# A tile of ones multiplied 32 times into an unread bank at the head of a single-core DiT block

## The chip, the cores and the metric

The kernel is one program on one core of a Trainium2 chip. The metric is the device time of one execution in microseconds (us); a kernel's number is the median over its runs. In a profile, PE is TensorE's matmul side and PEld its weight load, DVE is VectorE, ACT is ScalarE, POOL is GpSimd, and SP is the engine whose queue issues nearly all the loads.

## The reference

One layer of a diffusion block over 1024 latent tokens of width 1024, with 256 context tokens, all in float32:

```
sh1, sc1, g1, sh2, sc2, g2 = split(silu(c) @ w_mod + b_mod, 6)      # the same with c_ctx for the context
h  = rmsnorm(x, norm1_w) * (1 + sc1) + sh1                          # hc from ctx likewise
k, v, ig, fg, q, o, xin, gate_c, gate_b, merge = split(h @ w_in + b_in)
y_a = (gate_b * conv3(gate_c * xin)) @ w_conv_out
y_b = (norm(mlstm(q, k, v, ig, fg, state of hc)) * sigmoid(o)) @ w_mlstm_out
x  = x + g1 * ((sigmoid(merge_a) * y_a + sigmoid(merge_b) * y_b) @ w_out)
x  = x + g2 * (relu(modulate(x, norm2_w, sh2, sc2) @ w_ff1) ** 2 @ w_ff2)
out = rmsnorm(x, final_norm_w)
```

## The kernel before

Features lie on the 128 partitions and tokens along the free axis. Every large product is made of three products of halves (`PASS`): each operand is split into a high part and the rest (`whi`/`wlo`, `hh`/`hl`), and hi*hi, hi*lo and lo*hi are added in one bank. The conv, mLSTM-output, output and MLP products are cut into blocks with fewer multiplications (the `Pairs` class and its `m1` to `m7`).

This case is about the head of the program, some 47 us. It does, all at once:

- loads. `m` in the list `ORDER` loads one of 16 tiles `wmod` (512 KB each, half of the adaLN weights for one block of features), `x` one of the token tiles, `w` the first projection weights `wst`, `v` the weights `v0s`, `k` and `l` the constants and rows (`cst`, `comb`, `gb`, `vb`). All are issued by SP through the helper `dma` (line 92), in the written order.
- adaLN. `mod_rows(k)` (`r` in `ORDER`) multiplies two `wmod` tiles with `sil32`, the silu of both conditioning vectors padded to 32 columns: four column groups of 32, each 256 wide, into a bank `pso`. `y` copies the result to `mrow` on DVE; `mod_cols` (`c`) turns it into per-feature columns with eight very small products against `comb` into the one bank `psu` (`mcol`), and DVE makes `mod1` of them.
- the norm. `square` and `hat` (`h`, `n`) make the normalised tokens `xh` on ACT and DVE; `transposed` (`f`) transposes them on PE against `cst`; `modulate` (`u`) and `j` make `hh` and `hl`.
- the first projection. `gemm_k` (`g`) adds feature block after feature block into two banks `psg` with the weights of `w`.

`ORDER` fixes the order on every engine and queue: with `pinned[0]` true, each instruction is kept in program order (`tc.keep_in_program_order`); outside it the scheduler may place it. From some 47 us on the program is a long stream of products.

`bank()` gives a PSUM bank of 512 columns from a rotating pool of three (`psg`) in this part; `page()` gives a slot of SBUF from a pool of 37.

The program's first instructions, ahead of the change:

Of the kernel before, what the change touches and what calls it, by code (L numbers as in the profile page):

```python
# [13 lines left out]
P = 128  # L14
# [19 lines left out]
)  # L34
MOD_RATE = 0.16
YC = 448

U_K, U_Q, U_O, U_X, U_GC, U_GB, U_MA, U_MB = 0, 4, 8, 16, 24, 32, 40, 48
NUNIT = 56
# [19 lines left out]
def tile_block(ctx: ExitStack, tc: tile.TileContext, x, cx, w_mod1, w_mod, w_v0, w_v, w_unit, w_conv, w_mls, w_o, w_f1, w_f2, cols_d, rows_d, cst_d, out):  # L59
    nc = tc.nc  # L60
    pinned = [False]
# [18 lines left out]
    V, A, G, PE, SY = Engine(nc.vector), Engine(nc.scalar), Engine(nc.gpsimd), Engine(nc.tensor), nc.sync  # L80
# [17 lines left out]
    def nm(s):  # L98
        uid[0] += 1
        return f"{s}_{uid[0]}"  # L100

    def page(shape, dt=F32, name="pg"):
        return pg.tile(shape, dt, tag="pg", name=nm(name))
# [90 lines left out]
    def bank(tag="g"):  # L194
        if tag == "g":
            pool = psg
            if psg2:
                pool = (psg, psg2[0])[turn[0] % 8 > 2]
                turn[0] += 1
            return pool.tile([P, 512], F32, tag="g", name=nm("psg"))  # L200
        return psm.tile([P, 512], F32, tag=tag, name=nm("ps" + tag), bufs=2 if tag == "o" else 1)
# [6 lines left out]
    sil32 = page([P, 8, 32], name="sil32")  # L208
    G.memset(sil32, 0.0)
    V.tensor_copy(sil32[:, :, 0:2], sil)  # L210

    eps_c = cpool.tile([P, 1], F32, name="eps_c")
    V.memset(eps_c, EPS)
# [1519 lines left out]
    for j in range(4):  # L1733
# [27 lines left out]
        V.reciprocal(rs[:, 1:2], rs[:, 0:1])  # L1761
        yc = YC if t == TT - 1 else D
        A.activation(y[:, :yc], xf[:, :yc], AF.Copy, scale=rs[:, 1:2])
# [91 lines left out]
```

## Time and profile before

| what | value |
|---|---|
| median of 3 runs | 1772.45 us (1772.2 to 1773.82) |
| the profiled execution | 1773.45 us, of which the span is 1771.7 us |
| PE busy | 1724.8 us, 97% of the span |
| DVE, ACT, POOL busy | 71%, 42%, 10% |
| DMA | 261.10 MB, mean 147 GB/s; in the first of 40 slices 358 GB/s |

The span runs from the first to the last instruction; the execution's own time is 1.75 us longer. A slice of the page is 44 us, so the whole head is its first slice. In tables of stretches, `PEclk` is the clock that TensorE was granted, as a share of full speed, and the DMA share is the mean busy share of the 16 DMA engines.

### The profile page before, as it was taken

To read this page: it belongs to the slowest core of one execution; us is meant where nothing else is said; L and a number is where in the kernel's file an instruction comes from. 1 tells how busy PE (TensorE), PEld (TensorE's weight loads), DVE (VectorE), ACT (ScalarE), POOL (GpSimd) and SP (SyncE) were. 2 spreads that over 40 slices of the span, in tenths; PEclk is the share of its full clock that TensorE was granted. 3 is DMA by queue.
4 is the path that set the end of the run, shared out by engine and by line. 5 is a ranking of instruction groups with operands and counts; after the bars stand their busy time and mean duration, and the time that the engine had idled before them with its cause. 6 is when DMAs were issued, how large, how long until landed. Compare 5 with 4: busy or idle time off the path is not lost.

```text
span 1771.7 us, 23486 instructions
## 1 busy us (share of the span) xinstructions
PE 1724.8 (97%) x8633; PEld 1427.8 (81%) x8633; DVE 1252.1 (71%) x2216; ACT 745.5 (42%) x1229; POOL 177.6 (10%) x265
## 2 busy tenths in 40 slices
PE   6999999999999999999999999999999999999994
PEld 4998989877878888888888878877888888888884
DVE  4367556474966679878889988876666656577785
ACT  4534453565333322222344435554443454343434
POOL 1102221312200000000000001110111000000001
PEclk9999999999999999999999999999999999999997
DMA  9124131332525454343747255144344285675352
GB/s 358 47 61 105 34 90 44 89 81 63 201 96 172 161 166 137 102 162 110 262 157 258 71 215 175 64 166 161 133 164 161 107 287 193 233 240 189 106 179 95
DMA packets 102243, 261.10 MB, mean 147 GB/s; under 512 B 11760, under 2 KB 24944, under 8 KB 102128
## 3 DMA queue, kind: packets, MB, share of 16 engines
q1 hardware_dynamic: 85808, 200.88, 35.1%
q0 software_dynamic: 16320, 58.73, 8.4%
q8 instruction: 67, 1.10, 0.3%
q14 instruction: 48, 0.39, 0.1%
HBM read 198.62 MB, written 60.95 MB: 147 GB/s over the span
## 4 chain that ended last, share of the span: by engine, by line
PE 67%; DVE 3%; ACT 2%; issue 1%; ACTq 0%; DVEq 0%
PE psg L73 67%; ACT y L73 1%; DVE wst L73 0%; ACT Fsh L73 0%; DVE y L73 0%; ACT fc L73 0%; DVE fc L73 0%; DVE wlo L73 0%; DVE x L73 0%; DVE ftmp L73 0%; DVE Ff L73 0%; DVE Fsl L73 0%; DVE ol L73 0%; DVE f L73 0%; ACT fd L73 0%
## 5 line engine op out<-in xcount | busy, mean ns | idle before, releaser
L73 DVE TENSOR_TENSOR wlo<-wst,whi 128x512 fp32r<-128x512 f32 (+1 forms) x236 | 221.3, 941 | 143.4 <-ACT whi L73 141.3
L73 ACT ACTIVATE whi<-wst 128x512 fp32r<-128x512 f32 (+1 forms) x238 | 196.0, 827 | 259.8 <-PE psg L73 166.0
L73 PE MATMUL psg<-wlo,whi 128*128 128x512 f32 (+2 forms) x688 | 266.6, 387 | 0.2 <-DVE wlo L73 0.2
L73 PE MATMUL psg<-whi 128*128 128x512 f32 (+2 forms) x688 | 265.9, 387 | 0.0
L73 PE MATMUL psg<-whi,wlo 128*128 128x512 f32 (+2 forms) x688 | 265.4, 386 | 0.0
L73 PE MATMUL psg<-hh,whi 128*128 128x512 f32 x440 | 175.8, 406 | 0.0
L73 PE MATMUL psg<-hl,whi 128*128 128x512 f32 x440 | 172.4, 398 | 0.0
L73 PE MATMUL psg<-hh,wlo 128*128 128x512 f32 x440 | 172.0, 397 | 0.0
L73 PEld LDWEIGHTS psg<-whi 128*128 128x128 f32 x688 | 129.3, 188 | 27.8
L73 PEld LDWEIGHTS psg<-wlo,whi 128*128 128x128 f32 x688 | 129.2, 188 | 27.4 <-DVE wlo L73 0.6
L73 PEld LDWEIGHTS psg<-whi,wlo 128*128 128x128 f32 x688 | 129.2, 188 | 27.1
L73 PEld LDWEIGHTS psg<-hh,wlo 128*128 128x128 f32 x440 | 83.0, 189 | 18.9 <-DVE wlo L73 0.2
L73 PEld LDWEIGHTS psg<-hh,whi 128*128 128x128 f32 x440 | 82.1, 188 | 19.1 <-issue 0.8
L73 PEld LDWEIGHTS psg<-hl,whi 128*128 128x128 f32 x440 | 83.1, 189 | 16.9
L73 PE MATMUL psg<-oh,Fsl 128*128 128x512 f32 x240 | 94.7, 394 | 0.1
L73 PE MATMUL psg<-oh,Fsh 128*128 128x512 f32 x240 | 94.6, 394 | 0.0
L73 PE MATMUL psg<-ol,Fsh 128*128 128x512 f32 x240 | 94.6, 394 | 0.0
L73 DVE TENSOR_TENSOR u<-psg,u 128x512 f32<-128x512 f32 x67 | 45.8, 687 | 51.4 <-PE psg L73 51.4
L73 PE MATMUL psg<-whi,hh 128*128 128x256 f32 (+1 forms) x256 | 76.1, 297 | 0.0
L73 PE MATMUL psg<-whi,hl 128*128 128x256 f32 (+1 forms) x256 | 73.1, 286 | 0.0
L73 PE MATMUL psg<-wlo,hh 128*128 128x256 f32 (+1 forms) x256 | 73.1, 286 | 0.0
L73 POOL TENSOR_TENSOR wqz<-w,q 64x256 f32<-64x256 f32 x64 | 49.1, 771 | 158.6 <-PE pso L73 137.0
(338 smaller groups left out, 3797.5 us busy)
## 6 DMA issues: line engine op xcount, KB each, us to landing
wst<-fq SPq DMA_DIRECT2D x112, 256.0 KB, 2.7
wst<-in_w_unit_dram SPq DMA_DIRECT2D x38, 512.0 KB, 5.1
mst<-in_w_mod_dram SPq DMA_DIRECT2D x32, 512.0 KB, 4.4
fq<-Ff POOLq DMA_DIRECT2D x32, 512.0 KB, 3.7
wst<-in_w_f_dram SPq DMA_DIRECT2D x64, 256.0 KB, 3.0
wst<-in_w_f_dram SPq DMA_DIRECT2D x21, 512.0 KB, 4.4
Hwst<-in_w_unit_dram SPq DMA_DIRECT2D x18, 512.0 KB, 5.5
wmod<-in_w_mod_dram SPq DMA_DIRECT2D x16, 512.0 KB, 8.5
```

What stands on the lines that cost most here:

```text
L73: i = f(*a, **kw)
```

## The change

After `sil32` is made, a page of 128 by 128 ones is filled on DVE, and PE multiplies it with itself 32 times into 128 columns of a bank that nobody reads. The 32 products are pinned in program order, so they are the first work on PE.

```
+HUM = 32
...
     G.memset(sil32, 0.0)
     V.tensor_copy(sil32[:, :, 0:2], sil)
+
+
+    busy = page([P, P], name="busy")
+    V.memset(busy, 1.0)
+    hum = bank()
+    pinned[0] = True
+    for _ in range(HUM):
+        PE.matmul(hum[:, 0:P], busy, busy, start=True, stop=True)
+    pinned[0] = False
```

TensorE at the start of the program, before (`pso` from `wmod` and `sil` is `mod_rows`, `psm` and `pso` from `cst` and `xh` are transposes, `psu` is `mod_cols`):

```order
L73 MATMUL pso_169<-wmod_165,sil_2_83 32x256 x4
L73 MATMUL pso_169<-wmod_132,sil_2_83 32x256 x4
L73 MATMUL pso_186<-wmod_167,sil_2_83 32x256 x4
L73 MATMUL pso_186<-wmod_181,sil_2_83 32x256 x4
L73 MATMUL psm_55_204<-cst_67,xh_152 128x128
```

and now:

```order
L74 MATMUL psg_88<-busy_86 128x128 x32
L74 MATMUL pso_204<-wmod_200,sil_2_83 32x256 x4
L74 MATMUL pso_204<-wmod_167,sil_2_83 32x256 x4
L74 MATMUL pso_221<-wmod_202,sil_2_83 32x256 x4
L74 MATMUL pso_221<-wmod_216,sil_2_83 32x256 x4
L74 MATMUL psm_57_239<-cst_67,xh_187 128x128
```

The 32 products stand ahead of the first `mod_rows`; what follows is the same work in the same order, with other buffer numbers.

VectorE at the start of the program, before:

```order
L73 MEMSET eps_c 128x1
L73 MEMSET ones_c 128x2
L73 TENSOR_SCALAR kb_108<-cols 128x4
L73 TENSOR_TENSOR sil<-cols,sig 128x16
L73 COPY sil_2_83<-sil 128x8x2
```

and now:

```order
L74 MEMSET eps_c 128x1
L74 MEMSET busy_86 128x128
L74 MEMSET ones_c 128x2
L74 TENSOR_SCALAR kb_143<-cols 128x4
L74 TENSOR_TENSOR sil<-cols,sig 128x16
L74 COPY sil_2_83<-sil 128x8x2
```

One fill more, second on the engine; all other rows of DVE, and all rows of ACT, POOL and SP, follow each other as before.

## The prediction, made before the changed kernel had run

> **What bounds the kernel now.** I read the page's heading and engine shares first, then the list of what PE waited for, then a table of stretches of the head, then the rows of PE, DVE and SP there in order of time.
>
> ```profile
> span 1771.7 us, 23486 instructions
> PE 1724.8 (97%) x8633; PEld 1427.8 (81%) x8633; DVE 1252.1 (71%) x2216; ACT 745.5 (42%) x1229; POOL 177.6 (10%) x265
> PE pso L73 <- DMA wmod<-in_w_mod_dram: 13.6, 2, 11.6
> PE psg L73 <- ACT u L73: 1.5, 2, 1.2
> ```
>
> PE is busy for 97% of the span. Its waits are short but for one kind: 13.6 us in two pieces for tiles of `wmod`, the first of 11.6 us, from the start of the span. So whatever the change does must happen in the head, and it can reach the end only by letting the unbroken stream of products start earlier or run faster there.
>
> The head in stretches. I cut it where the granted clock changes (the column after POOL's; then the DMA share and GB/s):
>
> ```profile
> 0.00:10.90 10.90, 0.00 (x0) 0.00 (x0) 0.61 (x5) 4.93 (x8) 1.55 (x10) 1.00 0.84 313
> 10.90:14.32 3.42, 2.72 (x28) 1.37 (x32) 2.41 (x6) 3.32 (x9) 0.00 (x0) 1.00 1.04 402
> 14.32:17.73 3.41, 2.58 (x28) 1.85 (x20) 2.04 (x7) 0.19 (x1) 0.00 (x0) 1.00 1.02 407
> 17.73:21.14 3.41, 3.04 (x22) 1.37 (x21) 1.40 (x4) 1.93 (x3) 0.00 (x0) 0.50 1.02 414
> 21.14:24.56 3.42, 3.24 (x42) 1.90 (x43) 2.23 (x7) 0.92 (x1) 1.80 (x1) 1.00 0.88 347
> 24.56:27.97 3.41, 3.41 (x26) 3.04 (x24) 2.95 (x5) 2.05 (x4) 0.00 (x0) 1.00 0.87 339
> 27.97:31.38 3.41, 1.43 (x19) 0.83 (x19) 1.38 (x4) 1.71 (x3) 1.27 (x1) 1.00 1.03 420
> 31.38:34.80 3.42, 3.42 (x18) 2.64 (x20) 1.16 (x5) 0.01 (x1) 0.00 (x0) 0.50 1.03 419
> 34.80:46.60 11.80, 11.80 (x80) 8.80 (x73) 7.97 (x17) 9.19 (x15) 2.87 (x2) 1.00 0.65 260
> 100.00:1748.60 1648.60, 1640.26 (x8025) 1355.80 (x8023) 1197.99 (x2081) 682.32 (x1113) 157.60 (x237) 1.00 0.44 145
> ```
>
> Three things are to be seen. The DMA engines are full (share 0.84 to 1.04) until 34.8 us. The clock was granted at half speed twice, at 17.73 to 21.14 and at 31.38 to 34.80, each 3.4 us long and each right after a stretch of that length in which PE had gaps (2.58 and 1.43 of 3.41 us busy). And from 31.38 on PE has no gap: 3.42 of 3.42, then 11.80 of 11.80. What PE gains before its last long pause is lost again in that pause; what it gains behind it reaches the end.
>
> PE's rows there (start, length, then at the end of a row the idle time before it and what ended it):
>
> ```profile
> 11.60 3.25 PE L73 MATMUL pso<-wmod,sil 128*32 128x256 f32 x32 [11.60 <-DMA wmod<-in_w_mod_dram]
> 14.91 0.30 PE L73 MATMUL psm<-cst,xh 128*128 128x128 f32 x1
> 15.72 0.55 PE L73 MATMUL psm<-cst,xh 128*128 128x128 f32 x3 [0.52 <-DVE xh L73]
> ...
> 17.30 0.65 PE L73 MATMUL psu<-comb,mrow 128*128 128x2 f32 x4 [0.26 <-DVE mod L73]
> 17.81 1.10 PE L73 MATMUL psm<-cst,xh 128*128 128x128 f32 x4
> 18.84 1.94 PE L73 MATMUL pso<-wmod,sil 128*32 128x256 f32 x16
> 21.32 1.07 PE L73 MATMUL pso<-wmod,sil 128*32 128x256 f32 x16 [0.55 <-DVE mrow L73]
> 22.79 0.63 PE L73 MATMUL psm<-cst,xh 128*128 128x128 f32 x4
> 27.59 0.50 PE L73 MATMUL psu<-comb,mrow 128*128 128x2 f32 x4
> 30.08 1.07 PE L73 MATMUL pso<-wmod,sil 128*32 128x256 f32 x16 [1.98 <-DMA wmod<-in_w_mod_dram]
> 49.79 1.04 PE L73 MATMUL pso<-cst,xh 128*128 128x128 f32 x8
> ```
>
> The last pause ends at 30.08, with the landing of a `wmod` tile. That landing is not set by PE:
>
> ```profile
> SPq L92 <- DMA wmod<-in_w_mod_dram: 8.1, 9, 1.0
> SPq L92 <- DMA x<-in_x_dram: 3.3, 4, 1.1
> SPq L92 <- DMA wst<-in_w_unit_dram: 1.8, 2, 0.9
> L92 SPq DMA_DIRECT2D wmod<-in_w_mod_dram x9: 327/328/1168, 11.5 to 26.5; - x9
> 19.90 0.33 SPq L92 DMA_DIRECT2D wmod<-in_w_mod_dram  x1
> DMA to landing us min/median/max: 8.3/10.0/10.1
> ```
>
> The first three rows are all that SP's queue waited for before 26 us, beside 0.7 us at the start: earlier transfers, never PE, DVE or ACT. The product at 30.08 is the sixth `mod_rows` (`r5`), which needs tiles `m11` and `m10`; `m10`, the later, was issued at 19.90, and the longest 10.1 us to landing gives 30.0. So the whole line up to 30.08 is the DMA engines emptying a list at 400 GB/s.
>
> **The change part by part.** The fill of `busy`. Two fills of VectorE and one of GpSimd bound it:
>
> ```profile
> 0.80 0.06 DVE L73 MEMSET eps_c<- 128x1 f32 x1 [0.80 <-PEq L1845]
> 0.73 0.31 POOL L73 MEMSET sil<- 128x256 f32 x1 [0.29 <-POOLq L1845]
> 2.74 0.17 DVE L73 TENSOR_SCALAR kb<-cols 128x4 f32<-128x4 f32 x1 [1.85 <-DMA cols<-in_cols_dram]
> ```
>
> It is 128 columns on DVE, between 0.06 (one column) and 0.31 us (256 columns on a slower engine); I take 0.2. DVE has nothing to do from 0.89 until 2.74, where it waits for `cols`, so the fill costs nothing; if it took 2 us it would push `sil`, which is needed at 11.60. Fill and semaphore let PE begin at about 1.2 us.
>
> The 32 products. A float32 product that is no transpose leaves two rows in the trace: the 16 of the first two `mod_rows` are x32 at 11.60, while the four transposes at 22.79 are x4. So 64 rows, each 128 columns by 128. The nearest rows are the transposes of that shape: at full clock x8 take 1.04 and x4 take 0.63, 0.41/4 = 0.103 us a row; at half clock, x4 from 17.81 to the next start at 18.84, 0.26 at most, and 0.205 as twice 0.103. All at full clock is 64 x 0.103 = 6.6 us, all at half is 13.1 (16.6 by the 0.26). Which clock? The stretch table says 1.00 from the start, but its first recorded change comes later; the pace tells more. At 11.60, x32 in 3.25 is 0.102 a row; the same product is 1.94/16 = 0.121 at half clock and 1.07/16 = 0.067 at full. So the first products after an idle start ran mostly at half, and rose somewhere before 14.9. With 1.5 to 5 us of the ones at half clock (7 to 24 rows), the 64 rows end at 1.2 + 6.6 + half of that, 8.6 to 10.3 us. I take 9.5. PE's first needed product starts at 11.60 because its tile lands then; the ones are hidden wholly under that wait, with 2 us to spare. If that cover were gone, each further us would delay the first `mod_rows`.
>
> What the ones leave behind. The products at 11.60 can run at full clock: 32 x (0.102 - 0.067) = 1.1 us less of work. But the tiles for them land one by one. The transposes that follow wait for `xh` and constants, and began at 14.91, 0.06 us after the products' end at 14.85. Between 0 and 1.1 us can be gained at this place, and I take 0.4. Downstream it is absorbed: PE rests from 28.09 (27.59 + 0.50) until 30.08 for the DMA, so a gain of 0.4 makes that rest 2.4 us instead of 2.0. Worth at the end: 0.
>
> The same holds for a loss: with less work in 10.90 to 14.32, that stretch could be judged idle, and the half-clock stretch could come at 14.32 instead of 17.73. At most 3.41/2 = 1.7 us, of which 2.0 are free. Worth at the end: 0.
>
> The bank and the page. `hum` is one of three banks, first used otherwise by the projection at about 26 us; the slot of `busy` is free when the ones end. SP, ACT and POOL have their old order. I find no wait that this adds: 0.
>
> The rule that speaks against this change stands in the Trainium skill, "TensorE: Matmul & The Clock Gate", Part 1: the clock is decided anew from PE's activity in each window of some 3.4 us, and an idle one lets it fall back to half. The trace agrees: both half-clock stretches are 3.4 us long and follow a stretch with gaps. By that rule, work that ended at 9.5 says nothing about the clock at 17.73 or 31.38, and the sum by it is the same 0.
>
> Sum: 0 (fill) + 0 (ones, hidden) + 0 (first `mod_rows`, absorbed) = 0 on the profiled execution's 1773.45 us. That execution lay 1.00 us above the median of the runs, 1772.45; against that median I forecast 1772.4. Its own range: the half-clock stretch at 31.38 to 34.80 is the one cold time behind the last pause and costs 3.42/2 = 1.71 us. Where its borders fall against the pause can differ between executions (the three runs differ by 1.62 us), so 1771.0 to 1774.0.
>
> **The rivals.** First: the clock stays up. If the early work shifts PE's rows enough that the stretch around 27.97 to 31.38 no longer counts as idle (1.43 us busy before; the one at 14.32 with 2.58 also fell), the 1.71 us at 31.38 to 34.80 vanish: 1770.7. For it: PE is unbroken there, so every saved us counts. Against it: the pause in front of it is caused by DMA and grows if PE is faster. The Trainium skill, "TensorE: Matmul & The Clock Gate", "Why this matters for your kernels", asks for no pause of PE over some 3 us if throughput is not to drop; the one from the ones' end to 11.60 is 2 us and the later ones are no longer, so by that rule the clock would never fall, and the time would be this 1770.7. The trace disagrees: it fell at 31.38 after a rest of only 1.98 us.
>
> Second: the longer rest costs. PE comes to 28.09 earlier, rests longer, and starts at 30.08 at half clock: the 1.30 us from 30.08 to 31.38 become half speed as well, 0.65 us more: 1773.1. Still no change that can be told.
>
> Third, slower: the ones run long and late. All at half clock by the 0.26 they end at 1.2 + 16.6 = 17.8, 6.2 us after 11.60. The first `mod_rows` then lose their waits and run at full clock (1.1), the pauses of 0.52, 0.26 and 0.55 before 15.72, 17.30 and 21.32 give some 1.3, the rest at 28.09 gives 2.0: +1.8 us, 1774.2. They become measurably slower only if weight load and product don't overlap: weights and moving operand are the same tile. One transpose alone took 0.30 and its load 0.14:
>
> ```profile
> 14.88 0.14 PEld L73 LDWEIGHTS psm<-cst,xh 128*128 128x128 f32 x1 [0.51 <-DVE rs L73]
> ```
>
> 0.44 a row is 64 x 0.44 = 28.2, ending at 29.4, 17.8 late; less the same 4.4 of slack, +13.4 us, 1785.8. It decides from a row of (3.5 + 4.4 + 10.4)/64 = 0.29 us on. Against it: in every row of four or eight transposes the load lies under the product before.
>
> **How the numbers follow.** A change of 0.2% (3.5 us) is about what a measurement of this kernel can tell from none. Hidden and absorbed, 1772.4: 0.58. Clock stays up, 1770.7: 0.20. Longer rest costs, 1773.1: 0.10. The ones cold and late, 1774.2: 0.05. No overlap, 1777 to 1786: 0.04. Some gain over 3.5 us that no row here shows: 0.03. The range from 1770 (the second with 0.7 us of scatter) to 1775 (the fourth with 0.8) holds the first four, 0.93, less what the spread of the runs takes. Faster by over 0.2%: 0.03; within: 0.92; slower: 0.05.
>
> **What would show it.** Right: 64 rows of `psg<-busy` from about 1.2 to 9.5 us, the first third at twice the length of the rest; `mod_rows` at about 11.6 with some 0.067 us a row where its tile is there; the product behind the last pause still at 30.1, released by DMA; PE unbroken behind it. The step on the clock is wrong if 31.38 to 34.80 no longer holds a half-clock stretch, or holds two; the step on the DMA if that pause ends elsewhere than at 30.1; the whole if the ones end behind 14 us.

## The result, and the profile after

| kernel | median | runs | ratio to before, 95% interval |
|---|---|---|---|
| before | 1772.53 us | 22, 1771.67 to 1773.82 | |
| after | 1775.36 us | 22, 1774.82 to 1776.51 | 1.0017 [1.0011, 1.0022] |

The change costs 2.8 us, 1.9 to 3.9 by the interval: little, but clear of the noise. The median lies 0.4 us above the predicted range, which ended at 1775. The execution profiled of after took 1775.33 us, 0.03 below its median; that of before (1773.45) lay 0.9 us above its own, so the two spans (1771.7 and 1773.6) show only 1.9 of the 2.8.

The page of after, its span and engine shares:

```profile
span 1773.6 us, 23615 instructions
PE 1736.3 (98%) x8697; PEld 1436.4 (81%) x8697; DVE 1254.0 (71%) x2217; ACT 744.9 (42%) x1229; POOL 177.0 (10%) x265
```

PE has 64 rows more and 11.5 us more of busy time than before (1724.8). The ones are 9.95 of it (their row stands below); some 1.5 us are in the other 8633 rows, which are the same as before.

The head of after, cut where its clock changes (columns: stretch, length, PE, PEld, DVE, ACT and POOL busy with their rows, clock, DMA share, GB/s):

```profile
0.00:6.44 6.44, 5.36 (x25) 5.36 (x26) 0.76 (x6) 2.98 (x4) 1.55 (x10) 1.00 0.68 232
6.44:30.33 23.89, 18.38 (x175) 12.89 (x174) 12.14 (x29) 11.15 (x20) 1.27 (x1) 1.00 1.01 400
30.33:33.75 3.42, 3.11 (x19) 1.73 (x20) 1.70 (x3) 0.90 (x2) 1.28 (x1) 0.50 1.03 421
33.75:46.60 12.85, 12.77 (x86) 9.58 (x86) 8.82 (x17) 9.46 (x17) 2.58 (x2) 1.00 0.68 264
```

One half-clock stretch of the head is left of two, at 30.33 instead of 31.38, and the product that ends PE's last pause now runs inside it: 16 rows in 1.93 us, where before took 1.07. PE's rows with the ones and the pauses:

```profile
1.08 9.95 PE L74 MATMUL psg<-busy 128*128 128x128 f32 x64 [1.08 <-DVE ones_c L74]
11.54 1.83 PE L74 MATMUL pso<-wmod,sil 128*32 128x256 f32 x24 [0.51 <-DMA wmod<-in_w_mod_dram]
14.03 0.64 PE L74 MATMUL pso<-wmod,sil 128*32 128x256 f32 x8 [0.66 <-DMA wmod<-in_w_mod_dram]
...
27.52 0.50 PE L74 MATMUL psg<-hh,whi 128*128 128x512 f32 x1 [1.01 <-ACT whi L74]
...
30.64 1.93 PE L74 MATMUL pso<-wmod,sil 128*32 128x256 f32 x16 [1.02 <-ACT hh L74]
...
56.11 0.38 PE L74 MATMUL psg<-whi,hh 128*128 128x288 f32 x1
```

The ones lie under the wait for `wmod`, as predicted: they end at 11.03, and the first `mod_rows` starts at 11.54 (before: 11.60). PE is 0.56 us late at 30.64. The last row is the first 288-wide product behind a batch of transposes; before it stood later, and here is why (before, PE):

```profile
56.08 0.66 PE L73 MATMUL pso<-cst,xh 128*128 128x128 f32 x4 [0.73 <-ACT mtmp L73]
56.49 0.38 PE L73 MATMUL psg<-whi,hh 128*128 128x288 f32 x1
```

Before waited there 0.73 us for ACT. So at 56 us after is not behind but 0.38 us ahead (56.11 against 56.49). All of the loss comes later, in the long stream of products. Three operations of DVE that occur once and wait for PE's products mark it. Before:

```profile
113.11 0.23 DVE L73 COPY md<-psu 128x64 f32<-128x64 f32 x1
757.56 0.17 DVE L73 SCALAR_TENSOR_TENSOR m<-m,cols 128x8 f32<-128x8 f32 x1
1677.84 0.68 DVE L73 TENSOR_TENSOR ftmp<-psg,ua 128x512 f32<-128x512 f32 x1
```

and after:

```profile
112.75 0.23 DVE L74 COPY md<-psu 128x64 f32<-128x64 f32 x1
758.04 0.17 DVE L74 SCALAR_TENSOR_TENSOR m<-m,cols 128x8 f32<-128x8 f32 x1
1679.68 0.69 DVE L74 TENSOR_TENSOR ftmp<-psg,ua 128x512 f32<-128x512 f32 x1
```

After minus before is -0.36, +0.48, +1.84 us, and 1.9 at the end. It grows in both stretches between the marks. Compared one by one (the n-th 512-wide product of after against the n-th of before), the products show no jump but an uneven growth: 1.65 us arise between 510 and 860 us, 0.2 us between 1060 and 1450. In stretches where PE has no gap it shows as fewer products in the same time; before, PE (columns: stretch, length, busy and rows, clock, DMA share, GB/s):

```profile
600.00:900.00 300.00, 300.00 (x1320) 1.00 0.45 152
1250.00:1700.00 450.00, 450.00 (x1960) 1.00 0.52 182
```

and after:

```profile
600.00:900.00 300.00, 300.00 (x1316) 1.00 0.44 151
1250.00:1700.00 450.00, 450.00 (x1957) 1.00 0.53 182
```

Same clock, the DMA share within 0.01, no gap, and each product 0.35 to 0.7 ns longer (300/1316 less 300/1320; 450/1957 less 450/1960). The change issues nothing there. What can reach so far is what the added page and bank do to the places of other tiles: in the compiled programs 222 of 1125 SBUF tiles and 78 of 348 PSUM tiles lie elsewhere than before.

### The profile page after: what moved, and what is told of

The parts are those of the page before. It is cut to its first block, busy times and chain, and to the rows that moved or that the text cites. A ratio compares the mean times of both kernels' runs of the same rounds, so it can differ in the third digit from the quotient of the medians.

```text
span 1773.6 us, 23615 instructions
## 1 busy us (share of the span) xinstructions
PE 1736.3 (98%) x8697; PEld 1436.4 (81%) x8697; DVE 1254.0 (71%) x2217; ACT 744.9 (42%) x1229; POOL 177.0 (10%) x265
## 4 chain that ended last, share of the span: by engine, by line
PE 90%; DVE 5%; ACT 3%; DMA 1%; issue 1%; SPq 0%; POOL 0%; ACTq 0%; DVEq 0%; POOLq 0%
PE psg L74 84%; PE pso L74 4%; PE psm L74 1%; PE psu L74 1%; ACT y L74 1%; DMA wst<-in_w_unit_dram 1%; DVE e L74 1%; DMA wmod<-in_w_mod_dram 1%; DVE wlo L74 0%; DVE cs L74 0%; ACT hs L74 0%; ACT whi L74 0%; ACT Fsh L74 0%; DVE y L74 0%; SPq L93 0%
```

## The experiments

All were timed in five rounds against before, 11 runs each; before had 1772.34 us in the first four and 1772.2 in the rest, 33 runs each.

| kernel | ones | page | bank | median (runs) | ratio, 95% interval |
|---|---|---|---|---|---|
| ones in place | 32 | no | no | 1772.62 (1772.12 to 1773.13) | 1.0002 [0.9993, 1.0011] |
| bank only | 32 | no | yes | 1772.6 (1772.23 to 1773.21) | 1.0002 [0.9993, 1.0011] |
| page only | 32 | yes | no | 1775.75 (1775.1 to 1776.24) | 1.0019 [1.0011, 1.0028] |
| one product | 1 | yes | yes | 1773.63 (1772.34 to 1774.17) | 1.0007 [0.9999, 1.0016] |
| places only | 0 | yes | no | 1774.92 (1774.31 to 1776.9) | 1.0017 [1.0008, 1.0026] |
| 64 in place | 64 | no | no | 1772.37 (1771.85 to 1772.73) | 1.0 [0.9991, 1.0009] |
| no bias | 0 | no | no | 1771.69 (1771.09 to 1773.35) | 0.9997 [0.9988, 1.0006] |
| no bias, even | 0 | no | no | 1770.05 (1768.99 to 1770.43) | 0.9988 [0.9979, 0.9996] |

**One product.** `HUM = 1` instead of 32, the rest as in after.

```
-HUM = 32
+HUM = 1
```

> One product of ones instead of 32, with the page and the bank of the changed kernel: 78 PSUM tiles change their bank as there, 151 SBUF tiles move (88 tiles lie otherwise than in the changed kernel, since the page comes free sooner), and PE has next to nothing to do at the head. Theory A (SBUF places): slower than 1772.5, 1774 to 1776, though not by the same amount, as the places differ. Theory B (banks): 1775. Theory C (the ones themselves): 1772.5.

1773.63 us: between before and after, a little below the 1774 to 1776 expected if the places in SBUF decide, and its interval still holds 1. But the page comes free earlier, later tiles take other slots (151 tiles moved against before, 88 of them lie otherwise than in after), so this is a third layout and tells ones and layout apart only together with the next runs.

**Ones in place.** The 32 products read a tile that exists anyway and write into unused columns of the bank of `mcol`. They stand further down in the source, but are still PE's first work. All SBUF and PSUM tiles lie as before.

```
-    busy = page([P, P], name="busy")
+    busy = gt["wk"][:, 0:P]
     V.memset(busy, 1.0)
-    hum = bank()
...
-        PE.matmul(hum[:, 0:P], busy, busy, start=True, stop=True)
+        PE.matmul(mcol[:, 256:384], busy, busy, start=True, stop=True)
```

> The same 32 products of ones at the head, but the ones lie in a constant tile that is written later (gt_wk) and the result goes to unused columns of the bank of mod_cols: every tile keeps the SBUF place and the PSUM bank that it had before. Before is 1772.5 us, the changed kernel 1775.4. Theory A (moved SBUF tiles slow the long stream of products): 1772.3 to 1773.3, only the head's +0.6 us is left. Theory B (moved PSUM banks slow it): the same 1772.3 to 1773.3. Theory C (the ones themselves: their time on PE and the instruction fetches that they bring forward): 1775.4, the whole loss.

1772.62 us, no change. Its ones take 1.08 to 10.95 and its head is after's (`pso` behind the last pause at 30.63, released by ACT). DVE's three marks:

```profile
112.73 0.23 DVE L74 COPY md<-psu 128x64 f32<-128x64 f32 x1
756.71 0.17 DVE L74 SCALAR_TENSOR_TENSOR m<-m,cols 128x8 f32<-128x8 f32 x1
1677.02 0.69 DVE L74 TENSOR_TENSOR ftmp<-psg,ua 128x512 f32<-128x512 f32 x1
```

This profile is at its median, so it is the better yardstick: after is 0.02 us behind it at 113 us, 1.33 at 757, 2.66 at 1678 and 2.8 in the span (1773.6 against 1770.8). The products of ones, and all that they do to the head, are worth nothing that can be told (+0.3 us, from -1.2 to +1.9 by the interval); after loses its 2.8 us behind the same head.

**Page only and bank only.** The page as in after with the result in `mcol`'s bank; and the bank as in after with the operand in `gt["wk"]`.

```
     busy = page([P, P], name="busy")                # page only
+        PE.matmul(mcol[:, 256:384], busy, busy, start=True, stop=True)
...
+    busy = gt["wk"][:, 0:P]                         # bank only
     hum = bank()
+        PE.matmul(hum[:, 0:P], busy, busy, start=True, stop=True)
```

> The 32 products read a page of ones, as in the changed kernel, so 222 of 1125 SBUF tiles lie where they lie in the changed kernel; the result goes to unused columns of the bank of mod_cols, so every PSUM tile keeps its bank. Theory A (SBUF places): 1775.4. Theory B (banks): 1772.3 to 1773.3. Theory C (the ones themselves): 1775.4, as in the run with nothing moved.

> The 32 products write a bank from the rotating pool, as in the changed kernel, so 78 PSUM tiles change their bank; the ones lie in a constant tile, so every SBUF tile keeps its place. Theory A (SBUF places): 1772.3 to 1773.3. Theory B (banks): 1775.4. Theory C (the ones themselves): 1775.4, as in the run with nothing moved.

The page alone gives 1775.75, the whole loss; the bank alone 1772.6, none. The page-only kernel also speaks against the clock as the cause: its granted clock never fell in the head, where before ran two stretches of 3.4 us at half, and it was still the slowest of the first four. Its head where those two stretches lay:

```profile
18.00:30.00 12.00, 9.33 (x89) 5.92 (x88) 7.61 (x17) 5.61 (x8) 1.27 (x1) 1.00 0.99 378
30.00:36.00 6.00, 5.65 (x51) 4.02 (x52) 3.20 (x7) 1.95 (x4) 1.28 (x1) 1.00 1.02 419
```

**Places only.** No ones on PE at all. The page is held just as long as in after by 40 fills on GpSimd, so that every SBUF tile lies where after has it; the banks are as before. But for the fills, every engine has before's instructions in before's order.

```
-    hum = bank()
-    for _ in range(HUM):
-        PE.matmul(hum[:, 0:P], busy, busy, start=True, stop=True)
...
+    for _ in range(40):
+        G.memset(busy, 1.0)
```

> No ones on PE at all: a page is allocated as in the changed kernel and filled 40 times by GpSimd, which holds it long enough that all 1125 SBUF tiles lie exactly where they lie in the changed kernel; PSUM banks are those of before. Theory A (moved SBUF tiles slow the long stream): 1775 to 1776 against 1772.4 before, the whole loss without a single product of ones. Theory C (the ones themselves, their instruction fetch, the clock): 1772.4.

1774.92 us, +2.7 without a single added product (1775 to 1776 were expected if the places in SBUF decide). Its marks and one gap-free stretch (two views of the same kernel):

```profile
111.86 0.23 DVE L74 COPY md<-psu 128x64 f32<-128x64 f32 x1
757.36 0.17 DVE L74 SCALAR_TENSOR_TENSOR m<-m,cols 128x8 f32<-128x8 f32 x1
1679.07 0.68 DVE L74 TENSOR_TENSOR ftmp<-psg,ua 128x512 f32<-128x512 f32 x1
```

```profile
600.00:900.00 300.00, 300.00 (x1316) 1.00 0.43 152
1250.00:1700.00 450.00, 450.00 (x1957) 1.00 0.51 182
```

It starts 0.87 us ahead of the ones in place (111.86 against 112.73) and is 2.05 behind at 1678: 2.9 us lost between, with after's counts of 1316 and 1957 rows. This shows the cause: the places of tiles in SBUF, not the ones, the bank or the clock. From the trace I also worked out the mean distance between the starts of the 512-wide products of halves behind 60 us, some 5960 in each trace: before 230.96 ns, ones in place 230.98, bank only 230.96; after 231.47, page only 231.48, places only 231.47; one product 231.14. Half a nanosecond times 5960 is 3.0 us.

Which products lose can be read from the same traces and the addresses in the compiled programs, again after against before, one by one. For 649 of the 512-wide products, neither they nor the five before and the five behind them have a moved operand (moving, own weights, next weights): their spacing changed by -0.01 ns on average. The other 5308 are 0.57 ns longer, 3.05 us in all. While 535 of the 649 ran, VectorE, ScalarE or GpSimd worked on a moved tile, and they changed by 0.04 ns, less than its uncertainty of 0.05. So what counts are the operands of PE, not tiles that these engines touch; what transfers touch was not looked at. It is not each product's own operands alone: 1482 whose own three stayed, but with a moved one among those neighbours, are 0.83 ns longer.

**What in the places.** Slots of the page pool are 4128 bytes long, 64.5 times 64, so every second slot starts 32 bytes off a multiple of 64. In before, spacings are 230.2 ns where the moving operand and the next weights have the same remainder by 64 (65% of them), and 232.4 where not; in after 63% have it. By the share alone that is 0.06 of the 0.51 ns: in after the alike pairs themselves take 230.8 and the others 232.6. To test whether this remainder is the rule, the slots were made 4160 bytes (65 times 64) and one small tile padded, so that 99.7% have it. SBUF had no room for that. The v bias was left out (its tile and its load; a constant one is added in its place), and a control leaves out the bias alone.

```
-        vb = wm.tile([P, 256], F32, tag="vb", name=nm("vb"), bufs=1)      # no bias
+        vb = C("ones")[:, None, :].to_broadcast([P, 2, 128])
...
-        va = [page([P, 2, 4, 129], name="va") for _ in range(2)]           # even: this as well
+        va = [page([P, 2, 4, 130], name="va")[:, :, :, 0:129] for _ in range(2)]
```

> The control for the next run: the kernel before, with the tile of the v projection's bias (1 KB) left out and the constant ones added in its place, so that 1 KB of SBUF comes free and a transfer of 128 KB falls away per projection; the pages keep their stride of 4128 bytes, so that every second page starts 32 bytes off a multiple of 64. All theories: 1770 to 1773, near before.

> The same as the control, with a page stride of 4160 bytes and the work pool moved along, so that every operand of a product starts at a multiple of 64 bytes; order, waits and page numbers are those of the control. Theory A1 (in the trace of before, products whose moving operand and next weights start alike modulo 64 take 230.2 ns start to start, the others 232.4, 65% and 35% of 5958): the 35% lose up to 2.3 ns, 0.35 x 5958 x 2.3 ns = 4.8 us, so 3 to 7 us faster than the control. Theory A2 (places matter by something else than this remainder, such as how far apart two operands lie): within 2.5 us of the control, either sign. Theory C (places don't matter): the same as the control within 0.5 us.

The control has 1771.69, the even slots 1770.05: 1.64 us less, and the runs of the two don't overlap (1771.09 to 1773.35 and 1768.99 to 1770.43). If that remainder were the rule, 3 to 7 us were expected; within 2.5 if places matter by something else, and there it lies. First and last mark of the control:

```profile
111.56 0.23 DVE L73 COPY md<-psu 128x64 f32<-128x64 f32 x1
...
1675.76 0.68 DVE L73 TENSOR_TENSOR ftmp<-psg,ua 128x512 f32<-128x512 f32 x1
```

and of the even slots:

```profile
111.86 0.23 DVE L73 COPY md<-psu 128x64 f32<-128x64 f32 x1
...
1674.78 0.68 DVE L73 TENSOR_TENSOR ftmp<-psg,ua 128x512 f32<-128x512 f32 x1
```

1564.20 us between them against 1562.92: 1.28 us gained in the stream. But the products' mean spacing fell only from 230.97 to 230.80, not to the 230.2 of the pairs that were alike before. So the remainder by 64 is at most a part. Which addresses go badly together stays open: in the traces of before, page only and one product, the three addresses of a product (moving, its weights, the next weights) go with two thirds of the variance of the spacing (0.67 together, 0.64 corrected for the 1602 combinations of addresses that occur), and that remainder with 0.08. A version with even slots and the bias was not run, since SBUF lacks some 900 bytes for it; no run here beats before by more than 0.2%.

**64 in place.** As the ones in place, with `HUM = 64`, to see how much delay the head takes.

```
-HUM = 32
+HUM = 64
```

> 64 products of ones instead of 32, with every tile in its old place and bank: 128 rows, some 24 at 213 ns and 104 at 111 ns, so they end at about 18 us instead of 11 and the first mod_rows is some 6 us late. If the head has the 4.4 us of slack that the prediction counted, 1.5 to 2.5 us slower than with 32 in place (1774 to 1775); if the wait for the transfers hides it all, 1772.6; if there is no slack behind 11.6 us, 1778 to 1779.

1772.37 us, no change. PE:

```profile
1.08 17.24 PE L74 MATMUL psu<-gt_wk 128*128 128x128 f32 x128 [1.08 <-DVE ones_c L74]
18.25 1.93 PE L74 MATMUL pso<-wmod,sil 128*32 128x256 f32 x32
...
35.32 1.07 PE L74 MATMUL pso<-wmod,sil 128*32 128x256 f32 x16
...
56.42 0.38 PE L74 MATMUL psg<-whi,hh 128*128 128x288 f32 x1
```

The first `mod_rows` starts 6.65 us late (18.25 against 11.60) and the last row is level with before (56.42 against 56.49). The `mod_rows` that before has at 34.34 starts here at 35.32, 0.98 us late; the rest is made up by 56 us, where before waits for ACT. In this run the clock did not fall in the head, so part of the room may come from there.

## Why the prediction was wrong

- **The failed step: "The bank and the page", priced 0.** It looked for waits that the change adds and found none, and rightly: in after nothing waits for `busy`, and the bank alone is worth nothing. It did not ask what else moves when one page more is taken from a pool that rotates. The term belongs at +2.7 us (places only) to +3.4 (page only), and it is the whole error; the runs showed longer products there, 231.47 ns from start to start instead of 230.96, and no new wait. The order of instructions, which shows "the same work in the same order, with other buffer numbers", had the hint in it: the buffers lie elsewhere. The bank's half of the step stands: +0.3 us, from -1.2 to +1.9 by its interval.
- **Why the places looked free.** The Trainium skill, "TensorE: Matmul & The Clock Gate", Part 2, says that the next weights are loaded during the running product over a read port of their own, which takes nothing from the stream of the moving operand. By that rule alone the places would cost nothing and after would take before's time. The measurement decides: places only is 1.0017 [1.0008, 1.0026]. Whether the two reads meet somewhere or something else is slower, no run here tells.
- **The fill, hidden: right.** It took 0.17 us against 0.2 taken, in DVE's pause:

```profile
0.86 0.17 DVE L74 MEMSET busy<- 128x128 f32 x1
0.97 0.06 DVE L74 MEMSET ones_c<- 128x2 f32 x1
```

- **The 32 products, hidden: right in the mechanism.** 64 rows, the first at 1.08, worth 0 by the ones in place. Their end was mis-sized: 11.03 instead of 9.5, and outside the 8.6 to 10.3. 25 rows began in the first 6.44 us, 5.36/25 = 0.214 us a row where 0.205 was taken, and the slow part lasted 5.4 us, above the 1.5 to 5 assumed. The other 39 took (11.03 - 6.44)/39 = 0.118 on average. The cover left over was 0.5 us, not 2.
- **The first `mod_rows`: right.** It ended at 14.03 + 0.64 = 14.67 instead of 14.85, a gain of 0.2 us where 0 to 1.1 were expected, and nothing of it reached the end.
- **The pause that ends at 30.08 by DMA: wrong, without effect.** It ended at 30.64, by ACT. The first `wst` tile had come later (ACT, before, then after):

```profile
23.64 1.06 ACT L73 ACTIVATE whi<-wst 128x1024 fp32r<-128x1024 f32 x1 [2.51 <-DMA wst<-in_w_unit_dram]
```

```profile
24.91 1.06 ACT L74 ACTIVATE whi<-wst 128x1024 fp32r<-128x1024 f32 x1 [3.88 <-DMA wst<-in_w_unit_dram]
```

  The transfers, said to be independent of PE, moved by 1.3 us; why was not tested, and the no-bias control, which has no ones, also shows 24.58 here.
- **"What it gains behind it reaches the end": wrong.** The head has one more wait at 56.08, for ACT, which the reading stopped short of at 46.6 us. What PE gains in the head it waits for again there. Page only kept the full clock behind 7.02 us, and its wait there was 0.96 us, where before had 0.73:

```profile
56.18 0.66 PE L74 MATMUL pso<-cst,xh 128*128 128x128 f32 x4 [0.96 <-ACT mtmp L74]
```

  So the first rival's gain of 1.71 us would not have come either: 64 in place, with before's places and the full clock in the head, is no faster. A loss is covered there as well: the 0.56 us of after are gone by 56.11. The second rival's half speed did occur behind the pause (1.93 us for 1.07), and cost nothing. The third rival's slack of 4.4 us was too small: 6.65 us cost nothing, where by it 2.2 would have been lost.
- **The clock: half right.** One half-clock stretch stayed, 1.05 us from where the text had it, but it is worth nothing: 64 in place runs without it and is no faster. That the one at 17.73 would go was not foreseen. The runs don't tie either to the ones: places only and the no-bias control, without an added product, record no fall of the clock in the head at all.
- **The rivals.** A loss was looked for only in ones that run late or long and in a longer rest at half clock. The mechanism that decided was not among them, and the range ended where those did, at 1775.

## What to carry to other kernels

A tile added to a rotating pool changes the addresses of many tiles behind it, and in a kernel whose TensorE never rests this can be worth as much as the change itself: here 2.7 to 3.4 us of 1772, against 0 for the products. So give a trial a place that moves nothing else, or run the new layout without the new work as a control. And before calling an engine unbroken behind a point, read its waits on to the point where the head's delays are made up.

## What the runs showed of the hardware

- The pace of a stream of 128x512 products depends on where its operands lie in SBUF: 230.80 to 231.48 ns on average over five layouts, at the same granted clock and, in the stretches shown, without a gap. By one property of the addresses it is 230.2 against 232.4 ns in before, but that property explains little of the difference between layouts.
- The ones ran at little over half pace for 5.4 us, 0.214 us a row against 0.118 behind it, although the table of stretches shows a clock of 1.00 there. The trace's own record of the clock begins only at 6.44 us; before that, only the length of the rows tells.
